# Low parts of summed queries and keys on GpSimd, their scale in the copies from banks, and a changed order of values, second logits and weights in an attention unit

## The chip, the cores and the metric

The kernel runs on one core of one Trainium2 chip. The metric is the device time of one execution in microseconds, as the median of three runs. Engines are named as the profile does: PE multiplies matrices, PEld loads their weights, DVE is VectorE, ACT is ScalarE, POOL is GpSimd, and SP issues the DMAs, whose data travels over 16 DMA engines.

## What is computed

A trunk of two layers works on 1024 tokens of 1024 features: `x = x + rms_norm(mixer(rms_norm(x)))`, twice. The second layer is a state-space layer that this change does not touch. The first is attention with 16 heads of 64 features in three groups, (window, dilation) = (128, 1), (512, 4) and (2048, 16). Each group has its own queries, keys and values; their outputs are merged by a softmax over the three log-sum-exps, multiplied with a gate, and projected. The part that matters, shortened:

```python
proj = h @ w_in                     # queries, keys, values of 3 groups, and the gate's z
qkv, z = proj[..., :n_qkv].reshape(B, S, 3, 3, 16, 64), proj[..., n_qkv:]
for g, (window, dilation) in enumerate(DILATED_GROUPS):
    # each query sees the keys t - j*dilation, j = 0..window/dilation
    logits = einsum(q, k) * 64 ** -0.5 + bias          # 64 ** -0.5 = 0.125
    lse = logsumexp(logits)
    outs.append(einsum(exp(logits - lse), v)); lses.append(lse)
w = softmax(stack(lses), axis=0)
o = sum(w[..., None] * stack(outs))
return (o * silu(z)) @ w_out
```

## The kernel before

**Products of split numbers.** PE multiplies rounded float32 (`fp32r`). To keep accuracy, each operand is split into a high part, the rounded value, and a low part, the value less the high part; a product is then three matmuls (high by high, low by high, high by low). `split` (L101 to L108) does this: the high part is a copy on ACT (L104), the low part a subtraction on DVE (L105), or on the engine that is passed. With a scale, the high part is a scaled activation on ACT (L107), the low part one scalar_tensor_tensor on DVE, `src * scale - hi` (L108). In the profile a tile whose name ends in h is a high part, one that ends in l a low part (`qh`, `ql`, `kh`, `kl`, and `ph` for both halves of the probabilities).

**Attention units.** The attention runs in 24 units (`attn_units`, L868 on): 8 pairs of heads by 3 groups; unit m has pair m // 3 and group m % 3. A unit projects queries and keys with a block scheme that needs seven block products instead of eight: the two raw weight tiles `wraw` are combined by subtractions (`weights`, L537; the four subtractions are L546) into operands w1 to w6, each split in high and low part; ten `product` steps (L562) accumulate in two banks of PSUM, X (tile `x`: products 0, 2, 4, 6, 8) and Y (tile `y`); `sums` copies X out three times (L579: p1, u2, u3) and adds Y to these copies (L583). Of the queries one half is p1 and the other the final content of X, of the keys one half is u2 and the other u3. `qk` splits these: `qk 0` p1 and `qk 1` bank X with the scale 0.125, `qk 2` u2 and `qk 3` u3 without a scale. Product 0 of the next unit can only start when `qk 1` has read X.

Then a unit computes logits (L686, four quarters, in bank pair `psl`) and adds the bias and takes the maxima on DVE (L692, into `lg` and `ms`), negates the maxima (L703, `nm`), takes exponentials on ACT (L708), transposes the probabilities on PE (L714, `pt`), splits them (`ph`), and multiplies them with the split values `vs` (L763, `pso`). The values `vp` are loaded by `load_v` (L648), with the bias (L255), and split by `split_v`. `store` writes out through L782 and L783, `put_ms` sums and maxima (L796, L803).

**The order.** One pass of the loop (a period) interleaves four units: `cur` is projected, `one` (the unit before) gets its logits, the first half of its exponentials and PV, `two` the second half, and for `nxt` the weights are prepared. Every call goes through `Program` (`step`, L852), which makes the order of the code the order of the instructions on PE, ACT, DVE and GpSimd; SP issues all DMAs in its own order. GpSimd does the low parts of the weights and the four subtractions of every unit but the first, the rotations of a bias (L1607 on) once per pair, and the merge of the groups' outputs (L943, L944), whose weights `mw` come by DMA. Two `wraw` tiles exist, so the next unit's raw weights are asked for at a period's start.

In period m, the projected unit's ends are, in order: product 7, sums 7, logits 3 of `one`, T 0 0 and its split, `qk 0`, `qk 2`, product 8, `qk 1`, weights 4 of `nxt`, exps 1 0, product 9, sums 9, PV 0 0, T 0 1, `qk 3`, store 0 0.

Of the kernel before, what the change touches and what calls it, by code (L numbers as in the profile page):

```python
# [18 lines left out]
AF = mybir.ActivationFunctionType  # L19
ALU = mybir.AluOpType  # L20
# [25 lines left out]
def f32(ap):  # L46
    return ap.bitcast(F32)
# [52 lines left out]
def split(c, hi, lo, src, scale=None, engine=None):  # L100

    nc = c.nc
    if scale is None:
        c.last_hi = nc.scalar.copy(hi, src).ins  # L104
        return (engine or nc.vector).tensor_tensor(lo, src, f32(hi), op=ALU.subtract)  # L105
    else:
        nc.scalar.activation(hi, src, AF.Copy, scale=scale)  # L107
        nc.vector.scalar_tensor_tensor(lo, src, scale, f32(hi), op0=ALU.mult, op1=ALU.subtract)  # L108
# [150 lines left out]
def evac_q(c, ps, g, t0, q):  # L259

    n = ps.shape[1] // ORD[g]
    at = (S - t0) // ORD[g] - n
    hi, lo = (t.rearrange("p (r l) -> p r l", r=ORD[g])[:, :, at:at + n] for t in q)
    split(c, hi, lo, ps.rearrange("p (l r) -> p r l", r=ORD[g])[:, :, ::-1], 0.125)
# [44 lines left out]
class Quads:  # L309
# [4 lines left out]
    def __init__(self, c):  # L314
# [3 lines left out]
        def part(th, kh):  # L318
            return [t[:, 4 * kh:4 * kh + 4, :] for t in c.h[th]]

        add, sub = ALU.add, ALU.subtract

        def tt(o, x, y, op):
# [11 lines left out]

        t, r = c.vslot(8, F32), c.vslot(2, F32)
        tt(t, v[2][1], v[3][1], add)
        tt(t, t, v[2][0], add)
        tt(t, t, v[3][0], add)
        s1 = parts((4, 5), t)  # L340
# [18 lines left out]
    def quad(self, raw, order, product, banks, use):  # L359
# [33 lines left out]
        for i in order:  # L393
            w = weights(i)
            if accs[ACC[i]] is None:
                accs[ACC[i]] = banks(ACC[i])
            acc = accs[ACC[i]]
            product(i, self.rows[i], w, acc)
            self.done += 1
            for job in self.jobs.get(self.done, ()):  # L400
                job()
            with c.tc.high_priority(AHEAD):
                for b, ps in enumerate(acc):
                    p1, u2, u3 = (self.at(s, b) for s in self.sums)
                    if i == 0:
                        nc.scalar.copy(p1, ps)
                    elif i == 1:
                        t = c.slot("c11", tag="a")
                        nc.scalar.copy(t, ps)
                        use(0, 0, b, t)  # L410
                    elif i == 5:
                        nc.vector.tensor_tensor(u2, p1, ps, op=ALU.add)
                    elif i == 6:
                        nc.vector.tensor_tensor(u3, p1, ps, op=ALU.add)
                    else:
                        t, th, nh = {4: (u3, 1, 1), 3: (p1, 1, 0), 2: (u2, 0, 1)}[i]
                        nc.vector.tensor_tensor(t, t, ps, op=ALU.add)
                        use(th, nh, b, t)
# [87 lines left out]
class Unit:  # L506
# [30 lines left out]
    def weights(self, n):  # L537
        c = self.c
        q, k = self.raw
        if n == 0:  # L540
            self.w1 = self.halves(q[:, :, 0], "w")
        elif n == 1:
            self.w6 = self.halves(k[:, 1, 0].unsqueeze(1), "w6", c.attn)
            for o, x, y in ((q[:, 0, 0], k[:, 0, 0], q[:, 0, 0]), (k[:, 0, 0], k[:, 1, 0], k[:, 0, 0]),
                            (k[:, 1, 0], k[:, 1, 0], q[:, 0, 0]), (q[:, 1, 0], q[:, 1, 0], k[:, 1, 0])):
                self.engine.tensor_tensor(o, x, y, op=ALU.subtract)  # L546
        elif n == 2:
            self.w2 = self.halves(q[:, :, 1], "w")
        elif n == 3:
            self.w3 = self.halves(k[:, :, 0], "w")  # L550
        elif n == 4:
            self.w4 = self.halves(q[:, :, 0], "w")
        else:
            self.w5 = self.halves(k[:, :, 1], "w5", c.attn)
# [21 lines left out]

    def copy(self, name):
        t = self.c.slot(name, tag="a").rearrange("p (r l) -> p r l", r=ORD[self.g])
        self.c.nc.scalar.copy(t, self.order(self.X, name == "p1"))  # L579
        return t  # L580

    def add(self, t):
        self.c.nc.vector.tensor_tensor(t, t, self.order(self.Y, t is self.p1), op=ALU.add)  # L583

    def bank(self, n):
        c = self.c
# [39 lines left out]
    def qk(self, n):  # L626
        c, g = self.c, self.g
        if n == 0:
            self.q, self.k = ([c.attn.tile([P, S], F32R, tag=x + y, name=x + y, bufs=1) for y in "hl"] for x in "qk")
        if n == 1:  # L630
            evac_q(c, self.X, g, H, self.q)
            return
        src = (self.p1, None, self.u2, self.u3)[n]
        w = H // ORD[g]
        at = 0 if n == 2 else w
        hi, lo = (t.rearrange("p (r l) -> p r l", r=ORD[g])[:, :, at:at + w] for t in (self.k if n else self.q))
        split(c, hi, lo, src, None if n else 0.125)

# [167 lines left out]
def merge_load(c, p):  # L808
    cm, e, d = c.compact
    src = bass.AP(c.ms_dr.tensor, c.ms_dr.offset + p * 3 * 4096, [[32, 64], [2048, 6], [1, 32]])  # L810
    c.nc.sync.dma_start(cm.rearrange("p g m n -> p (g m) n"), src)
# [58 lines left out]
def attn_units(c, w_in):  # L870

    nc, tc = c.nc, c.tc
    units = [Unit(c, m) for m in range(24)]
    c.outputs = [[] for _ in range(8)]
    step = Program(c)

    units[0].load(w_in)
    for n in (0, 2, 1, 3, 4, 5):
        units[0].weights(n)
    for m in range(26):  # L880
        cur = units[m] if m < 24 else None
        one = units[m - 1] if 1 <= m < 25 else None
        two = units[m - 2] if m >= 2 else None
        nxt = units[m + 1] if m + 1 < 24 else None

        def run(*steps):
            for unit, name, *args in steps:
                if unit is not None:
                    step(getattr(unit, name), *args)

        if nxt:
            nxt.load(w_in)
        run((cur, "product", 0), (two, "split_weights", 0, 1), (cur, "sums", 0))
        if m:
            run((cur, "weights", 5))
        if one and one.g == 0:
            step(rotations, c, one.p, 0)
            step(rotations, c, one.p, 1)
        if two and c.merge is not None:
            if two.g == 0:  # L900
                step(merge_weights, c, c.merge)
            step(merge, c, c.merge, c.outputs[c.merge], two.g)
            if two.g == 1:
                c.merge = None
        run((two, "exps", 1, 1), (cur, "product", 1), (two, "PV", 0, 1), (two, "T", 1, 0), (two, "store", 0, 1),
            (two, "split_weights", 1, 0), (one, "logits", 0))
        run((cur, "product", 2), (cur, "sums", 2), (cur, "product", 3), (cur, "sums", 3),
            (two, "PV", 1, 0), (two, "T", 1, 1), (two, "store", 1, 0), (two, "split_weights", 1, 1), (one, "logits", 1),
            (cur, "product", 4), (cur, "sums", 4), (one, "exps", 0, 0), (cur, "product", 5), (cur, "sums", 5),
            (two, "PV", 1, 1))  # L910
        if two:
            c.pair = two.p
            step(put_ms, c, two.g, two.ms)
        run((two, "store", 1, 1))
        if one:
            step(one.split_v)
        if cur:
            cur.load_v()
        run((nxt, "weights", 0), (nxt, "weights", 1))
        run((one, "logits", 2), (one, "exps", 0, 1), (cur, "product", 6), (nxt, "weights", 2), (nxt, "weights", 3),  # L920
            (cur, "product", 7), (cur, "sums", 7), (one, "logits", 3), (one, "T", 0, 0), (one, "split_weights", 0, 0),
            (cur, "qk", 0), (cur, "qk", 2), (cur, "product", 8), (cur, "qk", 1), (nxt, "weights", 4), (one, "exps", 1, 0),
            (cur, "product", 9), (cur, "sums", 9), (one, "PV", 0, 0), (one, "T", 0, 1), (cur, "qk", 3), (one, "store", 0, 0))
        if two and two.g == 2:
            merge_load(c, two.p)
            if two.p < 7:
                step(merge_maxima, c)
                c.merge = two.p
            else:
                c.last = c.outputs[7]  # L930
# [38 lines left out]
def attention(c, a):  # L969
# [67 lines left out]
    c.psa, c.psx, c.psy = c.ps("psa", 1), c.ps("psx", 1), c.ps("psy", 1)  # L1037
    c.attn = c.es_attn.enter_context(tc.tile_pool(name="attn", bufs=1, side="right", reuse_waits="tile"))
    attn_units(c, a["w_in"])
    return h  # L1040

# [952 lines left out]
```

## Time and profile before

| | |
|---|---|
| median of 3 runs | 1684.44 us (1682.27 to 1687.77) |
| profiled execution | 1685.35 us |
| its span, first to last instruction | 1683.5 us |
| mean granted TensorE clock | 0.991 |
| busy: PE, PEld, DVE, ACT, POOL | 1624.6, 1373.6, 1126.8, 772.1, 601.0 us |

The span is what the trace shows; 1.85 us lie around it. "Busy" counts the time in which an engine executes, so PE stands at 97% of the span. By stages, with the busy time of PE, PEld, DVE, ACT and POOL (in brackets how many instructions), the granted clock, the DMA share and GB/s in each stretch:

```profile
0.00:300.00 300.00, 289.98 (x2034) 259.80 (x2034) 258.41 (x585) 94.66 (x144) 12.45 (x19) 0.98 0.42 136
300.00:375.00 75.00, 74.67 (x504) 64.52 (x503) 46.09 (x90) 27.81 (x60) 24.87 (x25) 1.00 0.47 134
1100.00:1480.00 380.00, 370.18 (x1954) 313.13 (x1954) 273.59 (x550) 148.54 (x318) 133.68 (x108) 1.00 0.62 182
1480.00:1683.00 203.00, 191.79 (x854) 158.38 (x854) 93.92 (x181) 58.20 (x108) 47.71 (x35) 0.98 0.45 143
```

Up to about 300 us come the normalised input, its combinations and the values' projection; the first units start in the second stretch; the stretch from 375 to 1100 us holds the other units; behind it come gates, the output projection and the state-space layer.

Rows of waits read "engine tile line <- engine tile line: total us, times, longest": who waited, and which instruction ended the wait. Rows of groups read "line engine operation out<-in count: least/median/most ns, first to last us". A row of one instruction begins with its start and its duration in us.

### The profile page before, as it was taken

The page shows a single profiled execution, that of the slowest core. Times are in us where ns is not written, and L with a number is a line of the kernel's source. Part 1 is how long each engine was busy: PE and PEld are TensorE (multiplying, and loading weights), DVE is VectorE, ACT ScalarE, POOL GpSimd, SP SyncE. Part 2 cuts the span into 40 slices and gives each one's busy share as a digit, 9 for nine tenths or more (in the row PEclk, how much of TensorE's full clock was granted, in tenths as well). Part 3 has the DMA queues.
Part 4 walks back from the last instruction along what each step waited for, and adds up shares of the span by engine and source line. Part 5 has one row for each costly group of instructions (what it writes and reads, how often), then busy time and mean ns, then how long its engine had stood idle before and what let it go on. Part 6 is the DMA issues. An engine that isn't in the chain of part 4 may idle for free.

```text
span 1683.5 us, 26823 instructions
## 1 busy us (share of the span) xinstructions
PE 1624.6 (97%) x9606; PEld 1373.6 (82%) x9606; DVE 1126.8 (67%) x2635; ACT 772.1 (46%) x1904; POOL 601.0 (36%) x507
## 2 busy tenths in 40 slices
PE   8999999999999999999999999999999999999998
PEld 6889999978887788788878878877788888878886
DVE  8799898846565665756666565667564799954533
ACT  5332232246565665565666556656254232334411
POOL 1000000063445555554556555441321355433121
PEclk8999999999999999999999999999999999999999
DMA  6223455442232233223223332335436988664432
GB/s 246 70 47 108 149 178 164 143 115 61 69 91 76 77 108 80 91 82 98 77 77 112 89 99 82 90 112 153 136 113 197 238 250 242 209 209 153 154 113 87
DMA packets 184717, 212.22 MB, mean 126 GB/s; under 512 B 42483, under 2 KB 138502, under 8 KB 184584
## 3 DMA queue, kind: packets, MB, share of 16 engines
q1 hardware_dynamic: 184584, 210.52, 41.6%
q8 instruction: 75, 1.23, 0.3%
q14 instruction: 58, 0.48, 0.1%
HBM read 153.51 MB, written 56.96 MB: 125 GB/s over the span
## 4 chain that ended last, share of the span: by engine, by line
PE 42%; DVE 16%; POOL 15%; issue 12%; DMA 8%; ACT 5%; SPq 1%; POOLq 0%; DVEq 0%; ACTq 0%
PE psq L440 10%; PE pso L1170 10%; PE psj L130 10%; POOL w L105 4%; PE y L562 3%; POOL wraw L546 3%; DVE kl L105 2%; PE x L562 2%; DVE ql L108 2%; PE psv L298 2%; DVE ph L105 2%; DMA mw<-wt_dr 2%; ACT lg L708 2%; DVE T L1696 2%; POOL O L943 1%
## 5 line engine op out<-in xcount | busy, mean ns | idle before, releaser
L105 POOL TENSOR_TENSOR w<-wraw,w 128x512 fp32r<-128x512 f32 x138 | 185.4, 1359 | 298.2 <-ACT w L104 297.9
L562 PE MATMUL y<-hh,w 128*128 128x512 f32 x672 | 225.9, 394 | 0.0
L708 ACT ACTIVATE lg<-lg,nm 128x128 f32<-128x128 f32 (+1 forms) x384 | 168.6, 442 | 69.1 <-DVE nm L703 68.4
L562 PE MATMUL x<-hh,w 128*128 128x512 f32 x384 | 139.3, 413 | 15.3 <-DVE ql L108 15.3
L562 PEld LDWEIGHTS y<-hh,w 128*128 128x128 f32 x672 | 126.8, 189 | 29.0
L562 PE MATMUL y<-hl,w 128*128 128x512 f32 x336 | 131.9, 392 | 0.0
L763 PEld LDWEIGHTS pso<-ph,vs 128*128 128x128 f32 x736 | 101.1, 190 | 29.5 <-ACT ph L104 11.8
L583 DVE TENSOR_TENSOR u<-u,y 128x512 f32<-128x512 f32 x72 | 49.2, 683 | 105.5 <-PE y L562 105.5
L763 PE MATMUL pso<-ph,vs 128*128 128x256 f32 (+1 forms) x736 | 107.5, 282 | 12.7 <-ACT ph L104 8.3
L692 DVE CUSTOM_DVE_ANT_0 lg<-psl,T 128x128 f32<-128x128 f32 (+1 forms) x384 | 110.5, 347 | 12.8 <-PE psl L686 10.7
L440 PE MATMUL psq<-whi,v 128*128 128x256 f32 x640 | 118.4, 282 | 0.0
L105 DVE TENSOR_TENSOR ph<-pt,ph 128x512 fp32r<-128x512 f32 (+2 forms) x160 | 93.9, 620 | 33.6 <-ACT ph L104 31.8
L104 ACT CAST w<-wraw 128x512 fp32r<-128x512 f32 x144 | 81.5, 582 | 62.5 <-POOL wraw L546 58.2
L1548 POOL TENSOR_TENSOR Ks<-Ks,O 128x16 f32<-128x16 f32 x8 | 4.0, 500 | 293.2 <-ACT Ks L1546 293.2
L130 PE MATMUL psj<-h1h,whi 128*128 128x512 f32 (+1 forms) x272 | 104.2, 388 | 1.6 <-ACT h1h L104 1.0
L130 PE MATMUL psj<-h1l,whi 128*128 128x512 f32 (+1 forms) x272 | 102.5, 381 | 0.2 <-DVE h1l L105 0.2
L562 PEld LDWEIGHTS x<-hh,w 128*128 128x128 f32 x384 | 72.5, 189 | 35.4 <-DVE ql L108 19.0
L440 PEld LDWEIGHTS psq<-whi,v 128*128 128x128 f32 x640 | 99.3, 188 | 1.8 <-issue 1.2
L440 PE MATMUL psq<-wlo,v 128*128 128x256 f32 x320 | 89.6, 281 | 1.3 <-DVE wlo L105 1.3
L104 ACT CAST whi<-v 128x1024 fp32r<-128x1024 f32 x35 | 36.8, 1050 | 113.0 <-PE psq L440 81.2
L105 DVE TENSOR_TENSOR kl<-u,kh 128x512 fp32r<-128x512 f32 x48 | 58.1, 1210 | 42.5 <-ACT kh L104 42.5
L1197 POOL TENSOR_TENSOR xr<-xr,y 128x512 f32<-128x512 f32 x30 | 38.1, 1293 | 130.6 <-DVE y L1196 91.9
(302 smaller groups left out, 4496.5 us busy)
## 6 DMA issues: line engine op xcount, KB each, us to landing
wraw<-in_w_in_dram SPq DMA_DIRECT2D x56, 512.0 KB
v<-in_w_v_dram SPq DMA_DIRECT2D x24, 512.0 KB
mw<-wt_dr SPq DMA_DIRECT2D x84, 128.0 KB
vp<-v_dr SPq DMA_DIRECT2D x16, 512.0 KB
wraw<-in_ssm_w_in_dram SPq DMA_DIRECT2D x16, 512.0 KB
v_dr<-v SPq DMA_DIRECT2D x30, 256.0 KB
ca_dr<-ca SPq DMA_DIRECT2D x32, 144.0 KB
CA<-ca_dr SPq DMA_DIRECT2D x8, 576.0 KB
```

Of the source, the lines that this page charges most:

```text
L104: c.last_hi = nc.scalar.copy(hi, src).ins
L105: return (engine or nc.vector).tensor_tensor(lo, src, f32(hi), op=ALU.subtract)
L130: nc.tensor.matmul(ps, w[n == 2][:, k * P:k * P + P], h[n == 1][:, k, :], start=first and k == 0 and m == 0, stop=m == len(order) - 1 and ...
L440: nc.tensor.matmul(o, r[x][:, k, ts], w[y][:, k, :], skip_group_check=True, start=i in (0, 4, 5) and t % 2 == k == n == 0, stop=k == 3 and ...
L546: self.engine.tensor_tensor(o, x, y, op=ALU.subtract)
L562: c.nc.tensor.matmul(ps, w[:, y, a, b * P:b * P + P], rows[x][:, ks + b, :], start=start and m == 0, stop=stop and m == 5, skip_group_chec ...
L583: self.c.nc.vector.tensor_tensor(t, t, self.order(self.Y, t is self.p1), op=ALU.add)
L692: nc.vector.tensor_tensor_reduce(self.lg[u, j][:, h], psl[:, h, o], self.bt[:, h, 256 - w:256], scale=1.0, scalar=-3.0e38, op0=ALU.add, op ...
L708: c.nc.scalar.activation(t, t, AF.Exp, bias=self.nm[:, h, b:b + 1], accum_out=ms[:, col:col + 1])
L763: nc.tensor.matmul(o, l, r, start=n == 0, stop=n == len(jobs) - 1, skip_group_check=True)
L1170: nc.tensor.matmul(ps, x[:, k, ts], y[:, k, cols], start=n == m == 0, stop=n == KT - 1 and m == len(todo) - 1)
L1197: nc.gpsimd.tensor_tensor(x[:, ns], x[:, ns], y, op=ALU.add)
```

## The change

It has three parts.

1. The low parts of p1, u2 and u3 (`qk 0`, `qk 2`, `qk 3`) move from DVE to GpSimd. Since the split of p1 no longer scales, the scale 0.125 goes into the copy of p1 from bank X (an activation with a scale in place of a copy) and into the addition of Y to p1 (a scalar_tensor_tensor in place of a tensor_tensor). The split of bank X (`qk 1`) stays on DVE with its scale.
2. The next unit's `weights 0` moves from behind `load_v` to ahead of product 5, `weights 1` from there to right behind `store 1 1`, ahead of logits 2. Two of the four subtractions go from `weights 1` to `weights 0`; their results are the same.
3. `split_v` of `one` moves from ahead of logits 2 to behind them, and `load_v` with it.

The number of instructions of PE, ACT and SP doesn't change; DVE has 72 fewer, GpSimd 72 more.

```diff
     def weights(self, n):
...
+        def sub(o, x, y):
+            self.engine.tensor_tensor(o, x, y, op=ALU.subtract)
+
+        b11, b21, b12, b22 = q[:, 0, 0], q[:, 1, 0], k[:, 0, 0], k[:, 1, 0]
         if n == 0:
             self.w1 = self.halves(q[:, :, 0], "w")
+            sub(b11, b12, b11)
+            sub(b12, b22, b12)
         elif n == 1:
-            self.w6 = self.halves(k[:, 1, 0].unsqueeze(1), "w6", c.attn)
-            for o, x, y in ((q[:, 0, 0], k[:, 0, 0], q[:, 0, 0]), (k[:, 0, 0], k[:, 1, 0], k[:, 0, 0]),
-                            (k[:, 1, 0], k[:, 1, 0], q[:, 0, 0]), (q[:, 1, 0], q[:, 1, 0], k[:, 1, 0])):
-                self.engine.tensor_tensor(o, x, y, op=ALU.subtract)
+            self.w6 = self.halves(b22.unsqueeze(1), "w6", c.attn)
+            sub(b22, b22, b11)
+            sub(b21, b21, b22)
...
     def copy(self, name):
         t = self.c.slot(name, tag="a").rearrange("p (r l) -> p r l", r=ORD[self.g])
-        self.c.nc.scalar.copy(t, self.order(self.X, name == "p1"))
+        if name == "p1":
+            self.c.nc.scalar.activation(t, self.order(self.X, True), AF.Copy, scale=0.125)
+        else:
+            self.c.nc.scalar.copy(t, self.order(self.X, False))
...
     def add(self, t):
-        self.c.nc.vector.tensor_tensor(t, t, self.order(self.Y, t is self.p1), op=ALU.add)
+        v, y = self.c.nc.vector, self.order(self.Y, t is self.p1)
+        if t is self.p1:
+            v.scalar_tensor_tensor(t, y, 0.125, t, op0=ALU.mult, op1=ALU.add)
+        else:
+            v.tensor_tensor(t, t, y, op=ALU.add)
...
-        split(c, hi, lo, src, None if n else 0.125)
+        split(c, hi, lo, src, engine=c.nc.gpsimd)
...
-            (cur, "product", 4), (cur, "sums", 4), (one, "exps", 0, 0), (cur, "product", 5), (cur, "sums", 5),
+            (cur, "product", 4), (cur, "sums", 4), (one, "exps", 0, 0), (nxt, "weights", 0), (cur, "product", 5), (cur, "sums", 5),
...
         run((two, "store", 1, 1))
-        if one:
-            step(one.split_v)
+        run((nxt, "weights", 1), (one, "logits", 2), (one, "split_v"))
         if cur:
             cur.load_v()
-        run((nxt, "weights", 0), (nxt, "weights", 1))
-        run((one, "logits", 2), (one, "exps", 0, 1), (cur, "product", 6), (nxt, "weights", 2), (nxt, "weights", 3),
+        run((one, "exps", 0, 1), (cur, "product", 6), (nxt, "weights", 2), (nxt, "weights", 3),
```

What this does to the order of three engines, in the period that projects unit 14 (777 to 813 us in the profile of before). First DVE, at the end of the period, from the split of the last probabilities of `T 0 0`; p_7465 is p1 and u_7563 and u_7622 are u2 and u3 of this unit, x is bank X. Before:

```order
L105 TENSOR_TENSOR ph<-pt,ph 128x512
L105 TENSOR_TENSOR ph<-pt,ph 128x256
L108 SCALAR_TENSOR_TENSOR ql<-p_7465,qh 128x8x64
L105 TENSOR_TENSOR kl<-u_7563,kh 128x8x64
L108 SCALAR_TENSOR_TENSOR ql<-x,qh 128x8x64
L703 TENSOR_SCALAR nm<-ms 128x8
L583 TENSOR_TENSOR u_7622<-u_7622,y 128x512
```

And in the changed kernel (its line numbers are up to 12 higher or 5 lower):

```order
L105 TENSOR_TENSOR ph<-pt,ph 128x512
L105 TENSOR_TENSOR ph<-pt,ph 128x256
L108 SCALAR_TENSOR_TENSOR ql<-x,qh 128x8x64
L715 TENSOR_SCALAR nm<-ms 128x8
L595 TENSOR_TENSOR u_7622<-u_7622,y 128x512
```

Two low parts have left DVE ahead of the one that reads bank X. On GpSimd the same period runs from the last part of a merge (O_7086) to the first of the next (O_6740); w are the next unit's weights, w_7679 (w_7674 after) is its w6, and the subtractions write into wraw. Before:

```order
L944 TENSOR_TENSOR O_7086<-O_7086,O_6357 128x1024
L105 TENSOR_TENSOR w<-wraw,w 128x512
L105 TENSOR_TENSOR w_7679<-wraw,w_7679 128x256
L546 TENSOR_TENSOR wraw<-wraw 128x256 x4
L105 TENSOR_TENSOR w<-wraw,w 128x512 x3
L105 TENSOR_TENSOR w_7845<-wraw,w_7845 128x512
```

After:

```order
L105 TENSOR_TENSOR w<-wraw,w 128x512
L541 TENSOR_TENSOR wraw<-wraw 128x256 x2
L105 TENSOR_TENSOR w_7674<-wraw,w_7674 128x256
L541 TENSOR_TENSOR wraw<-wraw 128x256 x2
L105 TENSOR_TENSOR w<-wraw,w 128x512 x2
L105 TENSOR_TENSOR ql<-p_7465,qh 128x8x64
L105 TENSOR_TENSOR kl<-u_7563,kh 128x8x64
L105 TENSOR_TENSOR w<-wraw,w 128x512
L105 TENSOR_TENSOR kl<-u_7622,kh 128x8x64
L105 TENSOR_TENSOR w_7845<-wraw,w_7845 128x512
```

Two subtractions now stand ahead of w6, and the three low parts stand around w4's, the last of them ahead of w5's, which belongs to the next period. On ACT, from the last exponentials of `exps 0 0` on; mt are the sums and maxima to be stored, vs the values. Before:

```order
L708 ACTIVATE lg,ms<-lg,nm 128x128
L803 COPY mt<-ptm 32x128
L782 COPY O_7440<-pso 64x8x64
L104 CAST vs<-vp 128x16x64
L104 CAST w<-wraw 128x512
L104 CAST w_7679<-wraw 128x256
```

After:

```order
L720 ACTIVATE lg,ms<-lg,nm 128x128
L104 CAST w<-wraw 128x512
L815 COPY mt<-ptm 32x128
L794 COPY O_7440<-pso 64x8x64
L104 CAST w_7674<-wraw 128x256
L104 CAST vs<-vp 128x16x64
```

The high part of w1 has moved ahead of the store's copies, and the values' behind that of w6.

## The prediction, made before the change was run

> **What bounds the kernel now.** I read the page first (engines, then the chain that ended last), then the stage in which every edit lies, then the waits of TensorE in it, and last the chain inside one unit.
>
> ```profile
> span 1683.5 us, 26823 instructions
> PE 42%; DVE 16%; POOL 15%; issue 12%; DMA 8%; ACT 5%; SPq 1%; POOLq 0%; DVEq 0%; ACTq 0%
> 375.00:1100.00 725.00, 697.96 (x4265) 577.72 (x4263) 454.81 (x1232) 442.90 (x1276) 382.27 (x324) 1.00 0.30 87
> ```
>
> The third line is the busy time of PE, PEld, DVE, ACT and POOL between 375 and 1100 us, about 22 of the 24 attention units. PE works 697.96 of 725 us at a granted clock of 1.00; no other engine passes 63%. So a gain can only come out of PE's gaps, 27 us here, plus what the modelled ends of matmuls hide. Who ends those gaps (window 330 to 1115; total us, times, longest):
>
> ```profile
> PE x L562 <- DVE ql L108: 15.3, 15, 1.7
> PE pso L763 <- ACT ph L104: 6.8, 7, 1.0
> PE pso L763 <- DVE ph L105: 2.7, 8, 0.3
> PE psl L686 <- DVE ms L692: 2.4, 3, 1.1
> PE psj L130 <- DVE nm L703: 1.4, 1, 1.4
> PEld x L562 <- DVE ql L108: 19.0, 15, 1.9
> PEld pso L763 <- ACT ph L104: 9.9, 7, 1.4
> PEld pso L763 <- DVE ph L105: 9.3, 20, 0.6
> PEld psl L686 <- DVE ms L692: 4.1, 4, 1.5
> PEld psj L130 <- issue: 1.6, 1, 1.6
> ACT w L104 <- POOL wraw L546: 58.2, 23, 3.7
> ACT lg L708 <- DVE nm L703: 65.5, 33, 4.8
> POOL O L943 <- DMA mw<-wt_dr: 43.6, 8, 8.7
> ```
>
> The PE rows are too low, since a late matmul's modelled span reaches back; the PEld rows (weight loads) are too high, since loads normally run ahead. The sums, 28.6 and 43.9 us, bound what lies open. Where do the waits on ql come from? The chain of waits around unit 14, piece by piece:
>
> ```profile
> 801.61 2.52 POOL w L105 x2
> ...
> 805.72 0.75 POOL wraw L546
> ...
> 807.01 0.58 ACT ph L104
> ...
> 807.62 1.02 DVE ph L105 x2
> 808.64 1.70 DVE ql L108
> 810.34 1.68 DVE kl L105
> 812.02 0.60 DVE ql L108
> ```
>
> ACT stands in order before the high part of w3, which needs GpSimd's four subtractions (L546); only then come ph, DVE's ph, the low parts of p1 and u2 (1.70 + 1.68 us), and last the low part of bank X, which frees X for the next unit's product 0:
>
> ```profile
> 777.24 0.60 PE L714 MATMUL pt<-identr,lg 128*128 128x128 f32 x4
> 777.72 0.50 PE L562 MATMUL x<-hh,w 128*128 128x512 f32 x1
> ...
> 808.79 0.61 ACT L107 ACTIVATE qh<-x 128x512 fp32r<-128x512 f32 x1
> ...
> 810.75 0.84 PE L714 MATMUL pt<-identr,lg 128*128 128x128 f32 x6
> 812.68 0.50 PE L562 MATMUL x<-hh,w 128*128 128x512 f32 x1 [1.08 <-DVE ql L108]
> ```
>
> At 777.72 nothing is late: product 0 starts 0.12 us before the transposes end. At 812.68 it could have started at 810.75 + 0.84 - 0.12 = 811.47; 1.21 us are lost where the PE row says 1.08, a factor of 1.12.
>
> **Part 1: low parts to GpSimd, scale into the copies.** Per unit DVE loses one ql<-p and two kl; GpSimd gains three subtractions. Their prices:
>
> ```profile
> L105 DVE TENSOR_TENSOR kl<-u,kh x48: 684/694/1786, 353.8 to 1112.2; 128x512 fp32r<-128x512 f32 x48
> L105 POOL TENSOR_TENSOR w<-wraw,w x138: 721/1302/2296, 346.1 to 1080.4; 128x512 fp32r<-128x512 f32 x115, 128x256 fp32r<-128x256 f32 x23
> L583 DVE TENSOR_TENSOR p<-p,y 128x512 f32<-128x512 f32 x24 | 16.5, 687 | 16.8 <-PE y L562 16.8
> L108 DVE SCALAR_TENSOR_TENSOR ql<-x,qh 128x512 fp32r<-128x512 f32 x24 | 16.3, 677 | 0.0
> ```
>
> Ahead of the X evacuation DVE sheds 1.70 + 1.68 = 3.38 us. It then waits only for qh<-x, which ends at 808.79 + 0.61 = 809.40; ql<-x ends near 809.40 + 0.68 = 810.1, ahead of 811.47 by 1.4 us. So here the whole loss goes even if ACT's wait for GpSimd stays. Term: 15 waits, 15.3 x 1.12 = **17.1 us** (bounds 15.3 and 19.0). Late next is PE itself: the transposes' end.
>
> With ql<-x the maxima's negation (nm) comes over 2 us sooner, and with it the exponentials, kh, and all ACT does after. The waits on ph are of that descent:
>
> ```profile
> 780.29 0.69 DVE L105 TENSOR_TENSOR kl<-u,kh 128x512 fp32r<-128x512 f32 x1 [1.96 <-ACT kh L104]
> ...
> 782.35 0.28 ACT L823 ACTIVATE cm<-cm 64x96 f32<-64x96 f32 x1 [1.61 <-DVE cm L822]
> ...
> 783.15 0.38 PE L763 MATMUL pso<-ph,vs 128*128 128x256 f32 x1 [0.98 <-ACT ph L104]
> ```
>
> At the seven merges ACT holds ph back behind the exponential of the merge, that waits for DVE, and DVE had waited for kl's kh. All of it moves forward by those 2 us and by kl's 0.69; the wait of 0.98 goes. Terms, in the middle of the two kinds of rows: ACT ph (6.8 + 9.9) / 2 = **8.4**; DVE ph (2.7 + 9.3) / 2 = **6.0**; the last unit's wait on nm, 1.4 to 1.6, **1.5**.
>
> The scale costs nothing to speak of: p1's addition becomes a scalar_tensor_tensor on a bank, and that form takes 677 against 687 ns; the copy with a scale is the ACTIVATE already used for qh<-x, off TensorE's path. The range holds 24 x 0.1 = 2.4 us either way for these.
>
> The kl of 694 ns takes 1786 in the worst case, when GpSimd works. [...]
>
> **What it adds on GpSimd.** 3 x 1.30 = 3.9 us per unit, 86 us over the window's 22 units: 382 + 86 = 468 of 725 us, 65%. Behind kl's last instruction in GpSimd's queue stand w5's low part and the merge; before kl stand w2, w3 and w4. Who waits: the next unit's first logits.
>
> ```profile
> 741.89 4.68 POOL L105 TENSOR_TENSOR w<-wraw,w 128x512 fp32r<-128x512 f32 x3
> ...
> 751.98 0.39 PE L686 MATMUL psl<-kl,qh 64*128 64x256 f32 x2
> ```
>
> Without any earlier start, ql and u2's kl go in between, so w4 ends at 746.57 + 2.60 = 749.17 and u3's kl at 750.5. PE would ask at 751.98 less the 0.9 it has gained: 751.1. That is in time by 0.6 us, and part 2 gives several more. Cost taken: 0. Bounds: a gain is excluded, since nothing waits for these parts earlier; the loss is in rival 3.
>
> **Part 2: weights two products sooner.** The high part of w1 goes ahead of product 5, two subtractions go with it, the other two stay with w6. Same count of instructions; the loads are issued where they were. GpSimd stood idle there. So w1's low part and two subtractions (1.30 + 2 x 0.74 us) are gone when w6 comes, and ACT's 58.2 us in 23 waits shrink, but not in the units of the third kind: there the merge waits for its weights' DMA (8 waits, 43.6 us), and GpSimd is free only when ACT already is. Worth on PE: 0 beyond part 1, as 811.47 showed; it is slack for kl and ph. Without that cover, rival 3. The load must land sooner by some 5 us; I take 0, as both raw tiles are asked for at the unit's start.
>
> **Part 3: values split behind the second logits.** DVE's reductions no longer stand behind vs; the banks of psl come free sooner: 2.4 to 4.1, **3.3 us**. vs now stands ahead of the sums of product 7 and of the last reductions; the next loads of values move behind it on SP's queue, and nobody waits for them for a unit. For late vs and whatever comes next I take off **3 us**.
>
> Sum: 17.1 + 8.4 + 6.0 + 1.5 + 3.3 - 3 = 33.3. The profiled execution took 1685.35 us, 0.9 above the median of 1684.44 and inside the runs' range. 1685.35 - 33.3 = **1652**.
>
> **Rivals.** *1, only X is freed.* ACT still holds ph back, because GpSimd's subtractions are still late and ACT is the in-order engine between; the ph and psl waits stay. For it: the third kind of unit keeps its ACT wait. Gain 15.3 to 19.0: 1666 to 1670. [...] *3, slower: logits wait for GpSimd.*
>
> ```profile
> L1126 POOL TENSOR_TENSOR fz<-fz,tz 128x512 f32<-128x512 f32 x8 | 14.8, 1858 | 59.0 <-DMA fz<-on_dr 44.3 <-DVE tz L1096 8.6 <-issue 6.1
> ```
>
> If the strided views of q and k cost more than w's plain tiles, as with fz (1.86 us), three of them add 1.7 us, and blocking by vs 1.3: kl ends at 753.5, 2.4 us after PE asks, if part 2 brings nothing. Per unit that is more than the 1.5 us gained (36.3 / 24), the point from which it decides; 24 x 0.9 = 21 us slower, 1707.
>
> **How the numbers follow.** Forecast 0.64 (1642 to 1663), rival 1 0.22, rival 2 0.07, rival 3 0.07. The range goes from all PEld rows (1685.35 - 43.9 = 1642, rounded up) to the ql row alone (1685.35 - 15.3 = 1670); it leaves out rivals 2 and 3 and a little at the lower end. A measurement tells 0.3% (5 us) from no change. Faster 0.86, same 0.07, slower 0.07.
>
> **What would show it.** Right: no PE row on ql; kl and ql<-p on POOL near 1.3 us; nm over 2 us sooner after the transposes; psl not waiting for POOL; PE over 98% busy from 375 on. ACT's wait on L546 falls but stays in the third kind. [...]

## The result, and the profile after

| | before | after |
|---|---|---|
| median of 4 runs each | 1686.11 us (1682.27 to 1688.38) | 1638.62 us (1634.66 to 1639.87) |
| ratio, with its 95% interval | 1 | 0.9717 [0.969, 0.9743] |
| profiled execution, its span | 1685.35, 1683.5 us | 1634.66, 1632.8 us |

The change makes the kernel 2.8% faster. That is the side that was forecast, by more than was forecast: 1638.62 lies 3.4 us below the lower end of the range, 1642.

The page of the changed kernel, its span, its chain that ended last, and (third line, from the table by stretches) the busy times of PE, PEld, DVE, ACT and POOL between 375 and 1060 us, the units now:

```profile
span 1632.8 us, 26979 instructions
PE 88%; DVE 6%; DMA 4%; issue 1%; POOL 1%; ACT 1%; SPq 0%; DVEq 0%; ACTq 0%; POOLq 0%
375.00:1060.00 685.00, 685.00 (x4289) 577.00 (x4289) 398.60 (x1185) 445.74 (x1280) 463.33 (x388) 1.00 0.32 93
```

PE is busy for 685.00 of 685.00 us. The chain that had 42% of PE in it has 88%. In the units nothing but PE's own work is left. POOL's share is 463 of 685, 68%; 65% was forecast. The waits from 330 to 1115 us in the same view as before:

```profile
POOL O L953 <- DMA mw<-wt_dr: 56.0, 14, 8.8
ACT lg L720 <- DVE nm L715: 36.5, 27, 2.9
ACT w L104 <- POOL wraw L541: 19.0, 7, 3.2
PEld pso L775 <- ACT ph L104: 1.9, 2, 1.0
PEld pso L775 <- DVE ph L105: 1.5, 4, 0.5
PE pso L775 <- ACT ph L104: 1.5, 2, 0.7
PE pso L775 <- DVE ph L105: 0.7, 2, 0.3
```

No row of PE on ql is left. ACT's waits on the subtractions fall from 58.2 us in 23 to 19.0 in 7; six of these lie in units of the third kind (units 5 to 20, where a merge stands ahead on GpSimd), one in unit 1. The end of a unit of the third kind, unit 14 (from the timeline; start, length, engine, operation):

```profile
780.04 0.62 ACT L104 CAST w<-wraw 128x512 fp32r<-128x512 f32 x1 [2.59 <-POOL wraw L541]
...
782.99 0.69 DVE L108 SCALAR_TENSOR_TENSOR ql<-x,qh 128x512 fp32r<-128x512 f32 x1 [0.79 <-ACT qh L107]
783.30 1.30 POOL L105 TENSOR_TENSOR ql<-p,qh 128x512 fp32r<-128x512 f32 x1
783.60 1.03 DVE L715 TENSOR_SCALAR nm<-ms 128x8 f32<-128x8 f32 x1
...
784.60 0.84 PE L726 MATMUL pt<-identr,lg 128*128 128x128 f32 x6
...
785.20 0.48 PE L567 MATMUL x<-hh,w 128*128 128x512 f32 x1
```

ACT still waits 2.59 us for GpSimd here, but the low part of bank X is done at 783.68, 1.52 us ahead of product 0, which starts 0.60 us behind the transposes' start. Before, that distance was 1.93 us (810.75 to 812.68).

Where did the 50.7 us of span go (47.5 in the medians; the profiled execution after is the shortest of its four)? Up to 1115 us PE's instructions stand in the same order in both traces, so the time from the start of each matmul to the start of the next can be compared pair by pair:

| place | us saved | forecast |
|---|---|---|
| ahead of product 0 (ql) | 19.8 | 17.1 |
| PV, waits on ph | 18.3 | 8.4 + 6.0 |
| logits (psl) | 2.6 | 3.3 |
| last unit, wait on nm | 1.6 | 1.5 |
| late vs and what comes next | 0 | -3 |
| stretches at half the clock, and small rests, in the units | 3.6 | 0 |
| ahead of unit 0 | 0.9 | 0 |
| behind 1115 us | 3.9 | 0 |

### The profile page after: what moved, and what is told of

Same layout as the page of the kernel before. It is cut to its first block, busy times and chain, and to the rows that moved or that the text cites. A ratio compares the mean times of both kernels' runs of the same rounds, so it can differ in the third digit from the quotient of the medians.

```text
span 1632.8 us, 26979 instructions
## 1 busy us (share of the span) xinstructions
PE 1606.7 (98%) x9606; PEld 1368.8 (84%) x9606; DVE 1060.0 (65%) x2563; ACT 773.9 (47%) x1904; POOL 689.7 (42%) x579
## 4 chain that ended last, share of the span: by engine, by line
PE 88%; DVE 6%; DMA 4%; issue 1%; POOL 1%; ACT 1%; SPq 0%; DVEq 0%; ACTq 0%; POOLq 0%
PE y L567 18%; PE psj L130 16%; PE x L567 13%; PE psq L440 10%; PE pso L1180 10%; PE pso L775 5%; PE psl L698 5%; PE pt L726 4%; PE psv L298 2%; PE psb L130 1%; DMA v<-in_x_dram 1%; DVE T L1706 1%; PE pst L147 1%; DVE T L1711 1%; PE pv L1699 1%
## 5 line engine op out<-in xcount | busy, mean ns | idle before, releaser
L105 POOL TENSOR_TENSOR w<-wraw,w 128x512 fp32r<-128x512 f32 x138 | 164.5, 1199 | 135.0 <-ACT w L104 130.3
L795 DVE TENSOR_TENSOR O<-O,pso 64x512 f32<-64x512 f32 x64 | 44.2, 691 | 89.6 <-ACT O L794 89.6
L775 PE MATMUL pso<-ph,vs 128*128 128x256 f32 (+1 forms) x736 | 100.1, 276 | 2.1 <-ACT ph L104 1.5
L104 ACT CAST ph<-pt 128x512 fp32r<-128x512 f32 (+2 forms) x160 | 78.4, 531 | 30.4 <-PE pt L726 28.6
```

Of the source, the lines that this page charges most:

```text
L775: nc.tensor.matmul(o, l, r, start=n == 0, stop=n == len(jobs) - 1, skip_group_check=True)
```

## The experiments

All columns in us. "Units" is the profile's time from product 0 of unit 0 to product 0 of unit 23, "rest" what follows; the last column is the mean length of a unit of the first, second and third kind (group 0, 1, 2), from unit 3 to 22. "Units" and "rest" come from one profiled execution each. Each ratio is to executions of the kernel before that ran beside that kernel; their medians lie between 1683.82 and 1686.45.

| kernel | median | ratio to before, interval | units | rest | by kind |
|---|---|---|---|---|---|
| before | 1686.11 | 1 | 738.90 | 610.05 | 31.44, 31.62, 35.81 |
| changed | 1638.62 | 0.9717 [0.969, 0.9743] | 697.75 | 601.46 | 29.88, 31.11, 31.65 |
| e1, part 1 | 1645.31 | 0.9762 [0.9747, 0.9778] | 704.01 | 601.55 | 30.06, 31.28, 32.29 |
| e2, parts 2 and 3 | 1660.51 | 0.9853 [0.9838, 0.9868] | 714.30 | 608.98 | 30.50, 31.11, 33.67 |
| e3, parts 1 and 2 | 1641.45 | 0.9738 [0.9724, 0.9753] | 700.90 | 602.83 | 30.03, 31.11, 31.97 |
| e4, parts 1 and 3 | 1639.79 | 0.9727 [0.9711, 0.9744] | 700.83 | 602.79 | 30.18, 31.11, 31.67 |
| e5, part 2 | 1659.63 | 0.984 [0.982, 0.986] | 714.98 | 608.64 | 30.67, 31.10, 33.57 |
| e6, part 3 | 1678.19 | 0.995 [0.9933, 0.9967] | 731.30 | 611.26 | 31.02, 31.50, 35.08 |
| e7 | 1641.11 | 0.9729 [0.9705, 0.9754] | 699.41 | 602.43 | 30.05, 31.11, 31.74 |
| e8 | 1654.10 | 0.9813 [0.9788, 0.9839] | 710.75 | 604.27 | 30.18, 31.11, 33.43 |
| e9 | 1649.01 | 0.9798 [0.9775, 0.982] | 706.42 | 606.39 | 30.20, 31.11, 32.43 |
| e10 | 1694.21 | 1.0054 [1.0034, 1.0074] | 750.57 | 605.16 | 30.73, 34.12, 34.62 |
| e11 | 1732.26 | 1.0286 [1.0267, 1.0304] | 780.27 | 613.09 | 33.26, 33.51, 37.23 |

**e1: part 1 alone.** Against the kernel before (the addition of Y, left out here, is as in the change):

```diff
-        self.c.nc.scalar.copy(t, self.order(self.X, name == "p1"))
+        if name == "p1":
+            self.c.nc.scalar.activation(t, self.order(self.X, True), AF.Copy, scale=0.125)
+        else:
+            self.c.nc.scalar.copy(t, self.order(self.X, False))
...
-        split(c, hi, lo, src, None if n else 0.125)
+        split(c, hi, lo, src, engine=c.nc.gpsimd)
```

> Part 1 alone (low parts on GpSimd, scale in the copies; order of weights and values as before). Theory A, the forecast's: what DVE does ahead of ql<-x sets the end of a unit, so no PE wait on ql is left (15.3 us in 15 waits before), the waits of pso on ph fall below 3 us in the PE rows (9.5 before), psl stays at 2 to 3 us; 1640 to 1648 us. Theory B: ACT, held by GpSimd's subtractions ahead of the high part of w3, sets the end of a unit; then the waits of pso on ph stay near 9 us, and of ql at least a third; 1660 to 1675 us. Slower than before, by over 5 us, would be the logits waiting for kl from a GpSimd that runs late.

The waits in its units, PE's first, then ACT's on the subtractions:

```profile
PE psl L693 <- DVE ms L699: 2.5, 4, 1.1
PE pso L770 <- ACT ph L104: 1.5, 2, 0.7
PE pso L770 <- DVE ph L105: 1.3, 5, 0.3
...
ACT w L104 <- POOL wraw L546: 56.1, 22, 4.0
```

ACT waits for GpSimd as long as before (56.1 us against 58.2), and yet every wait on ql is gone and those of pso on ph fall from 9.5 to 2.8 us: 34.9 of the 41.2 us in the units. Theory A holds: with DVE's own work ahead of bank X and ahead of nm gone, the waits go, and ACT's wait is covered. From start to start, as in the table of places, all 19.8 us ahead of product 0 go in e1, and 5.0 of the 18.3 ahead of PV stay. e5 shows that ACT's wait was a part of the cause as well.

**e2 and e5: the order alone, and part 2 alone.** Low parts on DVE as before. Part 2, against the kernel before, without the body of `weights`, which is that of the change (e2 also has `split_v` and `load_v` behind logits 2):

```diff
-            (cur, "product", 4), (cur, "sums", 4), (one, "exps", 0, 0), (cur, "product", 5), (cur, "sums", 5),
+            (cur, "product", 4), (cur, "sums", 4), (one, "exps", 0, 0), (nxt, "weights", 0), (cur, "product", 5), (cur, "sums", 5),
...
         run((two, "store", 1, 1))
+        run((nxt, "weights", 1))
...
-        run((nxt, "weights", 0), (nxt, "weights", 1))
```

> Parts 2 and 3 alone (weights sooner, values behind the second logits; all low parts on DVE with the scale as before). Theory A: the 3.4 us of DVE work ahead of ql<-x stay, ACT's w3 comes sooner only in two of three units; the PE wait on ql keeps half or more (8 to 15 us), psl falls below 1 us; 1668 to 1682 us. Theory B: ACT's high part of w3 no longer waits, ph and with it all of DVE's end of a unit come 2 us sooner; ql falls below 5 us; 1645 to 1660 us.

> Part 2 alone (weights sooner; low parts on DVE, values ahead of the second logits). Parts 2 and 3 together took 24.6 us from units 0 to 22 (738.90 to 714.30 us). If the two add up, with about 3 us for part 3 as between part 1 and the others: 21 to 22 us here, 1662 to 1667 us. If part 2 only helps with part 3 beside it: under 12 us, 1672 us or more. Waits of ACT on GpSimd's subtractions near 24 us instead of 58.

e2, at 1660.51 us, lies between its two theories: the wait on ql keeps 9.5 us, as A said, but the time is nearly B's. e5, at 1659.63 us, gained more than either of its two allowed. PE's waits in e2 (first two lines), then PE's and ACT's in e5, part 2 alone:

```profile
PE x L567 <- DVE ql L108: 9.5, 6, 2.2
PE psj L130 <- DVE nm L708: 2.5, 1, 2.5
...
PE x L567 <- DVE ql L108: 6.8, 6, 1.8
PE psl L691 <- DVE ms L697: 2.7, 6, 1.1
PE psj L130 <- DVE nm L708: 1.4, 1, 1.4
...
ACT w L104 <- POOL wraw L541: 23.8, 8, 4.0
```

So the prediction's value for part 2, nothing beyond part 1, is right only beside part 1. By itself it takes 23.9 us (738.90 - 714.98). Ahead of product 0 either edit is enough in the first two kinds of unit: with part 2 ACT splits w3 earlier, so ph and DVE's queue start sooner; with part 1 DVE's queue is shorter. What part 2 can't mend are the six waits of the third kind, where the merge keeps GpSimd late (33.57 against 31.65 us a unit). The two gains, 34.9 and 23.9, therefore don't add up: together 38.0 (e3).

Part 3 gains nothing beside part 2 alone: 0.7 us in the units (714.98 - 714.30), none in the medians. The waits of psl go, but in e2 those on ql are 2.7 us longer than in e5, in as many places, and the last unit's on nm 1.1.

**e3 and e4: one part left out.** e3 is the changed kernel with `split_v` and `load_v` ahead of logits 2:

```diff
-        run((nxt, "weights", 1), (one, "logits", 2), (one, "split_v"))
+        run((nxt, "weights", 1))
+        if one:
+            step(one.split_v)
         if cur:
             cur.load_v()
-        run((one, "exps", 0, 1), (cur, "product", 6), (nxt, "weights", 2), (nxt, "weights", 3),
+        run((one, "logits", 2), (one, "exps", 0, 1), (cur, "product", 6), (nxt, "weights", 2), (nxt, "weights", 3),
```

e4 is the changed kernel with `weights 0` and `weights 1` as they were (their body is left out here) and together behind `store 1 1`, ahead of logits 2:

```diff
-            (cur, "product", 4), (cur, "sums", 4), (one, "exps", 0, 0), (nxt, "weights", 0), (cur, "product", 5), (cur, "sums", 5),
+            (cur, "product", 4), (cur, "sums", 4), (one, "exps", 0, 0), (cur, "product", 5), (cur, "sums", 5),
...
-        run((nxt, "weights", 1), (one, "logits", 2), (one, "split_v"))
+        run((nxt, "weights", 0), (nxt, "weights", 1))
+        run((one, "logits", 2), (one, "split_v"))
```

> Parts 1 and 2 without part 3 (values split ahead of the second logits as before). Both theories: as the changed kernel but for the waits of psl on DVE's reductions, 2.4 us in the PE rows before; 1638 to 1643 us. If psl waits are not there either, part 3 bought nothing: 1636 to 1640 us.

> Parts 1 and 3 without part 2 (weights where they were). Theory A: part 2 is only slack, 1637 to 1643 us, no PE wait on ql. Theory B: ACT still waits for GpSimd's subtractions (58 us in all before) and holds ph: pso waits on ph stay at 5 us or more in the PE rows, 1650 to 1670 us. Rival 3 of the prediction: GpSimd, later by up to 5 us, delays kl, and psl waits for it; over 1660 us.

Each misses some 3 us in the units (700.90 and 700.83 against 697.75); the medians, 1641.45 and 1639.79, differ from the changed kernel's by less than its runs spread. e3 shows the waits of psl on ms that part 3 removes, 2.6 us in 6. e4 shows one wait of PE on a low part that GpSimd makes, 0.9 us:

```profile
PE psl L693 <- POOL kl L105: 0.9, 1, 0.9
```

**e6: part 3 alone.**

```diff
-        if one:
-            step(one.split_v)
+        run((nxt, "weights", 0), (nxt, "weights", 1))
+        run((one, "logits", 2), (one, "split_v"))
         if cur:
             cur.load_v()
-        run((nxt, "weights", 0), (nxt, "weights", 1))
-        run((one, "logits", 2), (one, "exps", 0, 1), (cur, "product", 6), (nxt, "weights", 2), (nxt, "weights", 3),
+        run((one, "exps", 0, 1), (cur, "product", 6), (nxt, "weights", 2), (nxt, "weights", 3),
```

> Part 3 alone (values split behind the second logits). Theory A: the waits of psl on ms (2.4 us before) go, but a unit's end is still set by the split of bank X, so a part is given back there: 1682 to 1686 us, no difference that can be told. Theory B, the terms add up: 1681 to 1683 us.

Both theories missed: 1678.19 us, about 8 us less than before (0.995). The waits of psl on ms are gone, and most others shrink as well: ql from 15.3 to 13.8, pso on ACT's ph from 6.8 to 4.5 us in PE's rows. Counted from start to start against the changed kernel, the gaps ahead of product 0 fall from 7.4 to 4.5 us in the first kind of unit and grow from 11.1 to 11.6 in the third and from 0.3 to 1.4 in unit 0; the last unit's wait on nm grows from 1.6 to 2.6. So part 3 does cost something where bank X's split still ends a unit, here and in e2; why it helps the first kind was not followed up.

**e7 and e8: low parts back on DVE, one or two.** Against the changed kernel, for e7 `n == 0` (p1), for e8 `n != 3` (p1 and u2):

```diff
-        split(c, hi, lo, src, engine=c.nc.gpsimd)
+        split(c, hi, lo, src, engine=None if n == 0 else c.nc.gpsimd)
```

> The changed kernel with the low part of p1 back on DVE (without a scale), the two kl on GpSimd. In the changed kernel ql<-x ends 2.2, 3.0 and 0.9 to 1.5 us ahead of the next product 0 (units of the first, second, third kind). Theory A: 0.69 us more ahead of it stay inside that margin everywhere; no PE wait on ql; 1635 to 1641 us. Rival: GpSimd, busy beside it, blocks the instruction to 1.3 to 1.8 us; then the third kind waits 0.1 to 0.9 us, 8 times: 1639 to 1646 us.

> The changed kernel with the low parts of p1 and u2 back on DVE, u3's on GpSimd. Theory A: 1.4 us more ahead of ql<-x, so the third kind of unit waits up to 0.5 us (8 times, 2 to 4 us), the others not: 1638 to 1645 us. Rival: blocked by GpSimd to 2 x 1.3 to 1.8 us, the third kind waits 1.2 to 2.7 us and the first up to 1.4: 1650 to 1665 us, and half-clock stretches come back.

e7 is within 2.5 us of the changed kernel; PE waits 0.3 us for ql, once. e8 is 15 us slower than the changed kernel, as the rival said, and its chain in unit 11 (third kind, from the timeline) says why (start, length, engine, operation):

```profile
693.34 2.55 POOL L105 TENSOR_TENSOR w<-wraw,w 128x512 fp32r<-128x512 f32 x2
...
694.67 1.76 DVE L105 TENSOR_TENSOR ql<-p,qh 128x512 fp32r<-128x512 f32 x1
...
696.09 1.46 POOL L105 TENSOR_TENSOR w<-wraw,w 128x512 fp32r<-128x512 f32 x1 [0.21 <-ACT w L104]
696.36 1.75 DVE L105 TENSOR_TENSOR kl<-u,kh 128x512 fp32r<-128x512 f32 x1
...
698.02 0.68 DVE L108 SCALAR_TENSOR_TENSOR ql<-x,qh 128x512 fp32r<-128x512 f32 x1
```

Two instructions whose median in this run is 0.68 us take 1.76 and 1.75 us here, while GpSimd works on w (693.34 to 695.89, and from 696.09 on); the one behind them, which reads a bank, takes 0.68. So by these rows moving both off DVE is worth an estimated 2 x 1.75 us, not 2 x 0.68, in the third kind of unit. A unit of the third kind is 33.43 - 31.65 = 1.78 us longer in e8, and one half-clock stretch is back in the units.

**e9 and e10: how much more GpSimd bears.** The changed kernel with the low part of u3 computed again, two more times in e9, four more in e10, which is shown:

```diff
         split(c, hi, lo, src, engine=c.nc.gpsimd)
+        if n == 3:
+            for _ in range(4):
+                c.nc.gpsimd.tensor_tensor(lo, src, f32(hi), op=ALU.subtract)
```

> The changed kernel with the low part of u3 computed three times over on GpSimd (2 x 1.3 us more per unit ahead of w5 and of the next logits). In the changed kernel u3's kl ends 3.2, 4.4 and 6.6 to 8 us ahead of the first logits that read it (units of the first, second, third kind; 1.3 us in unit 0). Theory A: 2.6 us stay inside that; only unit 0 loses 1.3 us; 1636 to 1643 us. Rival 3 of the prediction, GpSimd already near its limit: psl waits for POOL kl in most units, 1650 us or more.

> The same with four more (5.2 us per unit). By the margins above the first kind waits 2.0 us and the second 0.8 us, the third not: 8 x 2.0 + 8 x 0.8 = 22 us, 1656 to 1666 us, with psl waiting for POOL kl. If the merge or w5 behind it is what counts, the third kind loses too and the time is above 1670 us.

e9, then e10, the waits that tell:

```profile
PE psl L701 <- POOL kl L652: 1.7, 1, 1.7
ACT w L104 <- POOL wraw L541: 24.2, 8, 4.1
```

```profile
PE psl L701 <- POOL kl L652: 23.7, 16, 4.7
ACT w L104 <- POOL wraw L541: 39.5, 9, 6.9
```

The mechanism of rival 3 exists, and in e10 it makes the kernel 0.5% slower than before: 1694.21 us. But it needs more than the prediction gave it. With 2.6 us more a unit on GpSimd only unit 0's logits wait (1.7 us); with 5.2 us more 16 waits of 23.7 us come. Both kernels lose more than the margins gave (1649 where 1636 to 1643 was expected, 1694 where 1656 to 1666 was). In e9 some 7.5 us of the loss lie ahead of PV's matmuls, 4.6 of them in the third kind of unit. There GpSimd's subtractions come later still (ACT's wait is 3.75 us in unit 5, 3.10 in the changed kernel), ACT and DVE behind them, and ph with them. So the reading is that GpSimd has two readers that care, and that the subtractions are the first to suffer; no run takes the two apart.

**e11: gaps made on purpose.** The changed kernel with the low part of bank X computed seven times over on DVE:

```diff
             evac_q(c, self.X, g, H, self.q)
...
+            for _ in range(6):
+                c.nc.vector.scalar_tensor_tensor(lo, src, 0.125, f32(hi), op0=ALU.mult, op1=ALU.subtract)
```

> The changed kernel with the low part of bank X computed seven times over on DVE (6 x 0.68 = 4.1 us more ahead of the next product 0). By the margins of 2.2, 3.0 and 0.9 to 1.5 us PE then waits 1.9, 1.1 and 2.6 to 3.2 us: some 45 us in units 0 to 22, and more where the probabilities come later. [...] 1683 to 1700 us.

1732.26 us, above the expected 1683 to 1700, since I had added only PE's gaps: 53.1 us in 22 of them, and 29 us more in the units: 3 ahead of unit 1, 11 in PV's waits, the rest put down to the clock. Between 345 and 1075 us ten stretches of halved clock appear, where the changed kernel has none. One of them, from the table by stretches (PE, PEld, DVE, ACT, POOL, then the granted clock):

```profile
360.50:364.00 3.50, 1.18 (x5) 1.04 (x6) 2.67 (x4) 0.62 (x1) 0.93 (x2) 1.00 0.38 129
364.00:367.40 3.40, 3.40 (x9) 2.65 (x9) 0.00 (x0) 1.10 (x2) 2.69 (x3) 0.50 0.06 24
367.40:371.00 3.60, 3.60 (x24) 2.69 (x24) 1.26 (x7) 0.00 (x0) 3.52 (x4) 1.00 0.44 146
```

Behind a gap, 3.4 us hold 9 matmuls, where at full clock 3.6 us hold 24 (of mixed lengths). The same is seen in the kernel before, behind the wait of 1.68 us for ql at 516.38:

```profile
513.47:516.88 3.41, 1.73 (x14) 1.45 (x13) 3.41 (x5) 0.58 (x3) 1.51 (x2) 1.00 0.17 35
516.88:520.29 3.41, 3.41 (x9) 2.64 (x9) 1.50 (x4) 3.41 (x13) 0.00 (x0) 0.50 0.30 119
```

A matmul of 512 columns takes 0.43 us from start to start there (517.84 to 518.27) and 0.23 behind it (520.36 to 520.59), so such a stretch costs an estimated half of its length, 1.7 us.

## Why the prediction was right and wrong

**What bounds the kernel: right.** PE's gaps were what could be won, and all of them in the units were won: PE stands at 685.00 of 685.00 us.

**Part 1: mechanism right, size low.** e1 shows the mechanism by itself. The term for ql was 15.3 x 1.12 = 17.1 with bounds of 15.3 and 19.0; the matmuls' starts give 19.8. The factor came from one unit, 1.21 against 1.08, and the product 0 that it was measured against, at 777.72, where the prediction says that nothing is late, was itself late: it starts 0.16 us behind the last transpose's start, and in the changed kernel 0.03. These 0.13 us in some 22 units are the 2.7 us that the term lacks.

**The step that failed** is "Terms, in the middle of the two kinds of rows" for the waits on ph: 8.4 + 6.0 = 14.4, where the starts give 18.3. PEld's rows (9.9 + 9.3 = 19.2) were nearly the truth, PE's (9.5) half of it. A late matmul's modelled span reaches back over the gap, so PE's row shows the smaller part, here 9.5 of 18.3; the middle had no ground. With ql the sum was 6.6 us short.

**The 3 us taken off for late vs** don't appear beside part 1, where bank X's split is done 1.5 us early (unit 14) and part 3 is only a gain (e3). Without part 1 such a cost exists: 2.7 us on ql and 1.1 on nm in e2 against e5.

**What the sum put at nothing failed too.** The prediction worked at a clock of 1.00 and took what lies ahead of unit 0 and behind 1115 us as unchanged. In the units two half-clock stretches of 3.41 us each (at 516.88 and 981.09) went with the gaps ahead of them, an estimated 3.4 us. Behind 1115 us 3.9 us went. PE's instructions from there to the end take 567.8 us before and 563.9 after. They take 562.5 to 565.2 in e1, e3, e4 and e7, and 566.4 to 568.2 in e2, e5 and e6, where PE has the order of before up to the end, and in e8, e9 and e10. By estimate up to 1.7 us of the 3.9 lie with the clock: about 200 us ahead of the end 6.83 us stand at half of it before, 3.41 after. The longest wait of the gate and output stage changed its kind; before, then after:

```profile
PE pso L1170 <- DVE wol L105: 3.2, 1, 3.2
```

```profile
PE pso L1180 <- ACT gh L104: 2.1, 1, 2.1
```

PE's order behind 1115 us is another in the changed kernel (the same in e1, e3 and e4); the wait on wol stays with the order of before (4.2 us in e2, 4.0 in e5) and is back in e8 and e9 (3.7 and 3.5). What in part 1 shortens this stage was not tried and stays open. With the terms as measured, 42.3 us, and nothing off for vs, the time would have been 1643, just inside the range; what took it out are the 8.4 us that the sum put at nothing (3.6 in the units, 0.9 ahead of unit 0, 3.9 behind 1115 us). The lower end, all PEld rows, was therefore no bound. The upper end has two values in the prediction, 1663 in the forecast and 1670 where the range is explained; the time lies below both.

**Part 2 as pure slack: nearly right beside part 1** (e4, without it, is 3.1 us longer in the units, in the median no more than the runs spread), and wrong as a statement on part 2, which alone takes 23.9 us.

**The rivals.** *1* fell: in e1 ACT waits for GpSimd as before, and ph no longer makes PE wait. Its chain was there in the kernel before all the same, as e5 shows. *2*, that the offload gives nothing, fell: it gave most of the gain. e8 shows why: back on DVE the two instructions take 1.76 and 1.75 us beside GpSimd in a unit of the third kind, and what has left DVE can't be held up there. DVE's small nm still is: nm takes 1.03 us beside GpSimd's ql in the timeline above, against 0.15 before, where no row of GpSimd runs beside it:

```profile
812.54 0.15 DVE L703 TENSOR_SCALAR nm<-ms 128x8 f32<-128x8 f32 x1
```

All the same it starts 2.8 us sooner with respect to the transposes (1.00 us ahead of them instead of 1.79 behind) and ends 1.9 us sooner. *3* is real, but the point from which it decides lies higher, between 2.6 us more a unit (e9, still faster than before) and 5.2 (e10).

No run points to a faster version: in the units PE has almost no gap left, and every part that is taken out or put back costs something or changes nothing that can be told.

## What to carry to other kernels

Where an engine is busy 96% of a stage, as PE was here (697.96 of 725 us), and nothing else is near, the gain to expect of an edit is the engine's gaps; measure them from start to start between neighbouring instructions in the trace, since the wait rows of PE showed half of them here (9.5 of 18.3 us on ph). Of two edits that shorten two branches of one chain, try each alone before adding their gains. An instruction moved off an engine is worth its length in that place, with what blocks it there, not its shortest length (in e8 1.75 us, not 0.68). A range needs room for what the sum puts at nothing, here the clock and the stages behind the edit.

## What the runs showed of the hardware that was not expected

In these traces the granted clock fell to 0.50 for 3.4 us at a time behind gaps as short as 1.83 us ahead of product 0. Of PE's gaps ahead of product 0 (from start to start, less 0.12 us) in six traces (before, e2, e5, e6, e8, e11), those of 1.8 to 2.4 us were followed by such a stretch in 12 of 22 cases (1.83 us at 516.38 in the kernel before; three of 1.97 to 1.99 us in e5) and not in the others (1.83 us at 714.85 and 1.84 at 911.10 before). Of seven of 3.2 to 4.1 us in e11 six were, and none below 1.8 us was. One stretch stands behind gaps elsewhere: the other of the kernel before, at 981.09, has gaps of 1.1 us ahead of PV's matmuls and 0.6 us between them in front of it. PE was busy for 1.73 of the 3.41 us ahead of 516.88. What decides between gaps of one length was not shown. By these figures a gap of 2 us can cost an estimated 3.7: itself and the 1.7 of the stretch.
